# Moving matmul operands to other SBUF addresses, pairing split parts in one slot, and one wide multiply in the last norm

## The chip, the cores and the metric

The kernel runs on one core of a Trainium2 chip. The metric is the device time of one execution in microseconds (us), the median of several runs. Four engines compute: TensorE (PE in the profile; its weight loads are PEld), VectorE (DVE), ScalarE (ACT) and GpSimd (POOL). SyncE (SP) issues the DMAs.

## The reference, cut to what matters

One layer of a streaming encoder over 2048 prompt tokens and 32 sample tokens, width 1024, all in fp32:

```python
qa, ka, va, qb, kb, vb = split_proj(rmsnorm(h, g_attn), w_in)   # one projection, 3072 columns
oa = diff_attn(qa, ka, va, t5_table, lam)     # 4 heads: softmax map 1 minus lam * softmax map 2
ob = band_attn(qb, kb, vb, band_table)        # 8 heads, each 64-token chunk sees itself and 8 before
h = h + concat(rmsnorm(oa, subln_g), rmsnorm(ob, out_norm_b)) @ w_out
c = rmsnorm(h, g_mlp)
h = h + square(relu(c @ w_up)) @ w_down       # 4096 hidden
h = h + sigmoid(h @ w_ple_gate) * (p @ w_ple_proj)
y = rmsnorm(h, g_final)
```

The keys and values are outputs too.

## The kernel before

**Split operands.** Every large product is done in three passes of a fast fp32 format (`F32R`): each fp32 operand is split by `split` (L177, L182, L188) into a high part (a rounded copy, by ScalarE) and a low part (the rest, by GpSimd or VectorE). `mm3` (L220 to L222) then runs high x high, high x low and low x high into the same PSUM tile. Each matmul has a *stationary* operand (128 x 128, loaded by a weight load) and a *moving* operand (128 partitions x up to 512 columns). So nearly every tile in this text comes as a pair of parts.

**Tokens** are tiled in four blocks of 512, the last of 544 (512 + 32), which is worked as two halves of 272 (`SUBS`). Stages in order:

- *Projection* (`vwide`, `vtile`, `proj`). In `vwide` and `vtile`, which make the values, the activations `aH`, `aL` are stationary and the weights move: 512 columns wide in `vwide` (weight tiles `wh0`, `wl0`), 256 wide in `vtile` (weight tiles `wh`, `wl` of shape 4 x 256). In `proj`, which makes queries and keys, the weights are stationary and `aH`, `aL` move.
- *Attention* (`attn_a_pair`, `attn_b_pair`). Scores `s` move the keys `ka` or `kbt`. The weighted sum `o` of `attn_a_pair` (L723 to L725) has the values `v` stationary and the transposed probabilities `pH`, `pL` moving, 256 wide; `attn_b_out` (L883) moves `pb`, 512 wide.
- *Output projection and MLP* for blocks 0 and 1 (`outproj`, `mlp`), whose moving operands are in the pools `actq`, `hq` and `uq`; then for blocks 2 and 3, where `mlp7` computes the first MLP product with seven half-size products instead of eight (operands `cs`, made by `cparts`, or by `cstage` through DRAM and `cload`). From `oload(2, ...)` on, the parts `ou` (attention outputs), `hu` (gate input), `uh`, `ul` (MLP hidden) and `pT` are in the pool `uh` with its ring tag `u`.
- *Gate* (`gate`) and *last norm* (`final`) for each block, woven into the MLP of another block; those of block 3 end the program.

The order of the work on each engine is fixed when the program is built, by a scheduler that simulates times and gives out slots of the pools. A new tile waits for the release of the slot that it takes.

**Addresses.** A pool's bytes per partition are the sum of its rings (tag by tag, in order of first use, `bufs` slots each, rounded up to 32 bytes). Pools opened on the left are stacked upwards from the low end, pools with `side="right"` downwards from the top. Two tiles exist for their size alone: `edge` (24 floats, topmost on the right, so that the first right-hand pool ends at 229,248) and `round` (24 floats at the low end). The sums give these places; the *phase* is the start address modulo 256 bytes:

| moving operand | pool | start | phase |
|---|---|---|---|
| `wh0`, `wl0`, 512 wide | `wv0`, right | 159,328 + 2,048 i | 96 |
| `wh`, `wl`, 256 wide | `wp`, left, slots of 4,096 | 11,264 + 1,024 i | 0 |
| `pH`, `pL`, 256 wide | `a0` at 155,264; `a1` at 155,520, right | 206,720; 196,736 | 128 |
| `pb`, 512 wide | `b` at 156,672, right | 204,416 | 128 |
| `ou`, `hu`, `uh`, `ul`, `pT` | `uh`, right, 20 slots of 2,176 | 185,728 + 2,176 i | 0 and 128 in turn |
| `cs` of block 2, 256 wide | `cs`, right, slots of 4,352, 16 floats in | 75,968 | 192 |
| `cs` of block 3, 272 wide | `cs`, right | 75,904 + 1,088 k | 128, 192, 0, 64 |
| `aH`, `aL` (blocks 0 to 2), `cH`, `cL`, `hH`, `hL` | left | multiples of 256 | 0 |

**Last norm.** For each half of block 3 `final` has the eight tiles of `h` (1024 = 8 x 128 rows) multiplied by the scale `y`: tile 7 by VectorE (L1405), tiles 6 and 5 by GpSimd (`pool_tt`, L167), tiles 4 to 0 one by one by VectorE (L1413); tiles 4 to 7 go out in one DMA, tiles 0 to 3 in another.

Of the kernel before, what the change touches and what calls it, by code (L numbers as in the profile page):

```python
# [13 lines left out]
F32 = mybir.dt.float32  # L14
# [6 lines left out]
P = 128  # L21
# [13 lines left out]
BLK = 544  # L35
# [107 lines left out]


class Kern:
    def __init__(self, tc, a):
        self.tc = tc
        self.nc = tc.nc
        self.a = a
        self.nt = 3  # L150
        self.pieces = None

    def dma(self, dst, src):
# [455 lines left out]
    def attn_a_pair(self, g, j, ka, ba, pool, ps_s, ps_t, ps_o, late, first=None):  # L609
# [72 lines left out]
        for c0 in range(0, len(kts), 4):  # L682
            ch = kts[c0 : c0 + 4]
            v = pool.tile([P, 4, 2, P], F32R, tag="v", bufs=2, name="v")
            if samp:
                for i, kn in ch:
                    self.dma(
                        v[:kn, i].rearrange("p a b -> p (a b)"),
                        self.vS[0][SP + P * i : SP + P * i + kn, 256 * g : 256 * g + 256],
                    )  # L690
            else:
                nch = len(ch)
                ins = self.dma(
                    v[:, :nch].rearrange("p k a b -> p k (a b)"),
                    self.vS[0][P * c0 : P * (c0 + nch), 256 * g : 256 * g + 256].rearrange("(k p) c -> p k c", p=P),
                )
                if c0 == 8 and late:
                    with self.tc.issue_after(ins.ins):
                        late.pop(0)()
            pH = pool.tile([P, 4, 256], F32R, tag="pH", bufs=2, name="pH")  # L700
            pL = pool.tile([P, 4, 256], F32R, tag="pL", bufs=2, name="pL")
            for qi, w in enumerate(ws):
                nr = SS if samp else P
# [92 lines left out]
    def attn_b_pair(self, h, j, kt, v, kb, bb, q, t1, pool, ps_s, ps_t, ps_o, step, late):  # L796
# [9 lines left out]
        for qi, t in enumerate(tiles):  # L806
# [37 lines left out]
            def second(qi=qi, nr=nr, kts=kts, held=held, end=t is tiles[-1]):  # L844
                if qi == 0:
                    px.append(pool.tile([P, 6, 2, 256], F32R, tag="p", bufs=2, name="pb"))
                p = px[0]
                e = held[0]
# [65 lines left out]
    def oload(self, b, wk, up, out, r=None):  # L914
# [74 lines left out]
    def cparts(self, b, wk, cs, out, r):  # L989
# [34 lines left out]
    def cstage(self, b, up, out, r):  # L1024
# [5 lines left out]

        def parts(k, *which):
            for x, raw in which:
                t = up.tile([P, up.aw], F32R, tag="u", name="cst")[:, :n]
                self.split(t[:, :m], t[:, m:], raw, "act", "dve")
                self.dma(out[x][:, :, k], t.rearrange("p (i c) -> p i c", i=2))
# [134 lines left out]
    def mlp7(self, b, hh, box, ops, wk, up, mm, md):  # L1170
# [83 lines left out]
        for ch in range(DFF // (2 * P)):  # L1254
# [4 lines left out]
            for f in range(2):  # L1259
                us.append([up.tile([P, up.aw], F32R, tag="u", name=x)[:, :n] for x in ("uh", "ul")])  # L1260
            r0, r1 = tmp("r0", n), tmp("r1", n)
# [22 lines left out]
    def hparts(self, b, wk, up, out):  # L1284
        n, t0 = BN[b], 512 * b
        hH, hL = [[up.tile([P, BLK], F32R, tag="u", name="hu")[:, :n] for k in range(8)] for _ in range(2)]
        out.append((hH, hL))
# [7 lines left out]
    def ptile(self, b, up, wk):  # L1295
        n, t0 = BN[b], 512 * b
        pT = [[up.tile([P, up.aw], F32R, tag="u", name="pT") for _ in range(2)] for _ in range(2)]
        for k in range(2):
            raw = (
                up.tile([P, up.aw], F32, tag="u", name="praw") if wk is None  # L1300
                else wk.tile([P, BLK], F32, tag="tmp", bufs=self.nt, name="praw")
# [5 lines left out]
    def gate(self, b, h, up, act, md, wk=None, made=None, pT=None):  # L1307
# [13 lines left out]
        else:  # L1321
            hH, hL = [[up.tile([P, BLK], F32R, tag="u", name="hu")[:, :n] for k in range(8)] for _ in range(2)]
        if made is None:
            for k in range(8):
                self.split(hH[k], hL[k], h[:, k, :n], "act", "dve" if k % 2 else "pool")
        for dq in range(2):
            ph, pl = self.wunit(a["w_ple_proj"][dq], [2, 512])
            for d4 in range(4):
                d = 4 * dq + d4
                wh, wl = self.wunit(a["w_ple_gate"][d], [8, P])  # L1330
                for s0, sn in SUBS[b]:
# [5 lines left out]
                    sg = (  # L1337
                        up.tile([P, up.aw], F32, tag="u", name="sig") if wk is None
                        else wk.tile([P, BLK], F32, tag="tmp", bufs=self.nt, name="sig")
# [28 lines left out]
    def final(self, b, h, wk, mm):  # L1368
# [22 lines left out]
        for s0, sn in SUBS[b]:  # L1391
# [14 lines left out]
            for k in range(6, -1, -1):  # L1406
                hv = h[:, k, sub]
                if not end:
                    nc.vector.scalar_tensor_tensor(hv, hv, self.g_final[:, k : k + 1], y, op0=ALU.mult, op1=ALU.mult)  # L1409
                elif k in (5, 6):  # L1410
                    self.pool_tt(hv, hv, y, ALU.mult)
                else:
                    nc.vector.tensor_tensor(hv, hv, y, op=ALU.mult)  # L1413
# [296 lines left out]
```

## Time and profile before

| | |
|---|---|
| median of 3 runs | 3025.55 us (3023.77 to 3027.49) |
| the profiled execution | 3025.88 us, of which its span is 3023.8 us |
| mean granted TensorE clock | 0.990 |
| TensorE busy | 2925.0 us, 97% of the span, 17217 matmuls |
| GpSimd, VectorE, ScalarE busy | 1887.1, 1823.2, 1746.1 us |

The span runs from the first to the last instruction. [...]

### The profile page before, as it was taken

Reading aid. Unit: us, or ns where it says so; the run is one execution under the profiler, and the core shown is the slowest. Engines: PE = TensorE matmul, PEld = TensorE weight load, DVE = VectorE, ACT = ScalarE, POOL = GpSimd, SP = SyncE. Lnnn points to the kernel's source line nnn. Section 1 sums busy time; section 2 is a strip of 40 time slices with the busy share of each in tenths; the row PEclk is TensorE's granted clock in tenths of the full one; section 3 lists DMA queues with packets and bytes.
Section 4 is the critical chain, followed back from the end, with each engine's and each line's share of the span. In section 5 each row is a group of like instructions: output and inputs, shape, how many; then the busy total and the mean of one; then the engine's idle time right before and its main releaser. Section 6 shows DMA issues by size and latency. Waiting matters only on the chain. (4 is left out here: it accounts for less than half of the span.)

```text
span 3023.8 us, 49919 instructions
## 1 busy us (share of the span) xinstructions
PE 2925.0 (97%) x17217; PEld 2576.6 (85%) x17217; DVE 1823.2 (60%) x4217; ACT 1746.1 (58%) x3226; POOL 1887.1 (62%) x2509
## 2 busy tenths in 40 slices
PE   8999999999989999999999999999999999999997
PEld 6798889999877888888888888778788887999997
DVE  5256554676565554667566566445677885677664
ACT  5365554777666665655665655554655455555455
POOL 2568775323465444666655655787688888787774
PEclk9999999999999999999999999999999999999999
DMA  9877867987887453655643543446423446323231
GB/s 311 283 235 237 242 205 220 272 238 223 251 251 219 136 152 105 188 150 168 207 143 124 149 141 111 157 157 209 162 91 134 142 142 239 129 91 119 98 103 54
DMA packets 295204, 528.45 MB, mean 175 GB/s; under 512 B 36316, under 2 KB 159232, under 8 KB 294952
## 3 DMA queue, kind: packets, MB, share of 16 engines
q1 hardware_dynamic: 294952, 525.27, 55.7%
q8 instruction: 136, 2.23, 0.3%
q14 instruction: 116, 0.95, 0.1%
HBM read 424.66 MB, written 104.45 MB: 175 GB/s over the span
## 5 line engine op out<-in xcount | busy, mean ns | idle before, releaser
L177 POOL TENSOR_TENSOR wl<-wr,wh 128x256 fp32r<-128x256 f32 x632 | 472.0, 780 | 246.2 <-ACT wh L182 218.3
L182 ACT ACTIVATE piece<-wr 128x512 fp32r<-128x512 f32 x406 | 245.4, 624 | 290.4 <-PE ups L221 131.2
L177 POOL TENSOR_TENSOR piece<-wr,piece 128x256 fp32r<-128x256 f32 x404 | 338.2, 862 | 93.5 <-ACT piece L182 87.0
L182 ACT ACTIVATE wh<-wr 128x1024 fp32r<-128x1024 f32 x228 | 240.0, 1055 | 200.2 <-PE ups L221 42.6
L167 POOL TENSOR_TENSOR wl<-wr,wh 128x256 fp32r<-128x256 f32 x280 | 216.6, 805 | 202.1 <-ACT wh L182 199.9
L220 PE MATMUL dps<-uh,piece 128*128 128x272 f32 (+1 forms) x768 | 246.7, 325 | 10.3 <-ACT piece L182 6.8
L167 POOL TENSOR_TENSOR piece<-wr,piece 128x256 fp32r<-128x256 f32 x280 | 237.2, 879 | 18.2 <-ACT piece L182 14.9
L222 PE MATMUL dps<-uh,piece 128*128 128x272 f32 (+1 forms) x768 | 247.1, 324 | 1.5 <-POOL piece L167 1.0
L221 PE MATMUL dps<-ul,piece 128*128 128x272 f32 (+1 forms) x768 | 247.0, 323 | 0.1
L221 PE MATMUL ups<-cs,piece 128*128 128x256 f32 (+1 forms) x864 | 244.8, 283 | 0.0
L220 PE MATMUL ups<-cs,piece 128*128 128x256 f32 (+1 forms) x864 | 244.8, 283 | 0.0
L222 PE MATMUL ups<-cs,piece 128*128 128x256 f32 (+1 forms) x864 | 244.7, 284 | 0.0
L220 PE MATMUL qps<-aH,wh 128*128 128x512 f32 (+1 forms) x640 | 227.4, 356 | 5.8 <-DVE ql L502 4.2
L221 PE MATMUL qps<-aL,wh 128*128 128x512 f32 (+1 forms) x640 | 227.2, 355 | 0.0
L222 PE MATMUL qps<-aH,wl 128*128 128x512 f32 (+1 forms) x640 | 226.7, 355 | 0.0
L665 ACT ACTIVATE e<-e,nm 128x128 f32<-128x128 f32 (+16 forms) x136 | 157.2, 1156 | 109.6 <-DVE nm L663 109.1
L1150 DVE TENSOR_TENSOR h<-h,dps 128x512 f32<-128x512 f32 x256 | 173.1, 681 | 69.0 <-PE dps L222 67.8
L1193 DVE TENSOR_TENSOR h<-h,dps 128x272 f32<-128x272 f32 (+1 forms) x384 | 188.8, 513 | 42.3 <-PE dps L222 41.7
L220 PE MATMUL dps<-uh,wh 128*128 128x512 f32 x512 | 204.7, 400 | 5.6 <-DVE h L1150 4.5
L220 PE MATMUL ups<-cH,wh 128*128 128x512 f32 x512 | 202.5, 396 | 0.0
L222 PE MATMUL ups<-cH,wl 128*128 128x512 f32 x512 | 202.3, 395 | 0.0
L221 PE MATMUL ups<-cL,wh 128*128 128x512 f32 x512 | 202.2, 395 | 0.0
(312 smaller groups left out, 9139.7 us busy)
## 6 DMA issues: line engine op xcount, KB each, us to landing
wr<-w_up SPq DMA_DIRECT2D x128, 512.0 KB, 3.5
wr<-w_down SPq DMA_DIRECT2D x128, 512.0 KB, 3.5
q<-qS SPq DMA_DIRECT2D x128, 256.0 KB, 5.2
v<-vSa SPq DMA_DIRECT2D x64, 512.0 KB, 4.6
wr<-w_qk SPq DMA_DIRECT2D x50, 512.0 KB, 5.0
ka<-kS SPq DMA_DIRECT2D x32, 512.0 KB, 7.4
wr<-w_out SPq DMA_DIRECT2D x32, 512.0 KB, 4.5
wr<-w_ple_gate SPq DMA_DIRECT2D x32, 512.0 KB, 4.1
```

What stands on the lines that cost most here:

```text
L167: nc.gpsimd.tensor_tensor(out[:, sl], a[:, sl], b[:, sl], op=op)
L177: nc.gpsimd.tensor_tensor(out[:, sl], a[:, sl], b[:, sl], op=op)
L182: nc.scalar.activation(hi, raw, AF.Copy)
L220: nc.tensor.matmul(ps, lh, rh, start=start and i == 0, stop=False)
L221: nc.tensor.matmul(ps, lh, rl, start=False, stop=False)
L222: nc.tensor.matmul(ps, ll, rh, start=False, stop=stop and i == n - 1)
L665: nc.scalar.activation(row, row, AF.Exp, bias=nmx, accum_out=z[:nr, m : m + 1])
L1150: nc.vector.tensor_tensor(hv, hv, ps, op=ALU.add)
L1193: nc.vector.tensor_tensor(hv, hv, ps, op=ALU.add)
```

## The change

The `edge` tile grows from 24 to 56 floats, so every right-hand pool begins lower. Unused gap tiles are put ahead of and behind `pH`, `pL` in the pools of `attn_a_pair` (48 and 80 floats) and of `pb` in that of `attn_b_pair` (96 and 32 floats), and 120 floats ahead of `xt` in `pp0`. `wh` and `wl` get slots of 4,608 bytes, in which a 4 x 256 tile starts 48 floats in. `cs` operands of block 2 start 48 floats into their tile instead of 16. The ring `u` of pool `uh` has 10 slots of 4,608 bytes instead of 20 of 2,176: a new class `Even` gives both parts of a split tile out of one slot, at floats 64 and 576 for widths to 512, at 32 and 608 for 544. A tile that is no part of a pair (`praw`, `sig`) takes a whole slot. In the last norm of block 3 GpSimd scales tiles 5 and 4, VectorE tiles 7 and 6, and then tiles 0 to 3 in one instruction with `y` broadcast.

```diff
+def pairs(up, count, w, name):
+    if isinstance(up, Even):
+        t = [up.pair(w, F32R, name) for _ in range(count)]
+    else:
+        t = [[up.tile([P, w], F32R, tag="u", name=name) for _ in range(2)] for _ in range(count)]
+    return [[p[i] for p in t] for i in range(2)]
+
+class Even:
+    whole = False
+    def __init__(self, pool, aw):
+        self.pool, self.aw = pool, aw
+    def pair(self, w, dt, name):
+        t = self.pool.tile([P, 1152], dt, tag="u", name=name)
+        return [t[:, o : o + w] for o in ((32, 608) if w > 512 else (64, 576))]
+    def tile(self, shape, dt, tag, name):
+        return self.pair(shape[1], dt, name)[0]
...
-            hi = self.wp.tile([P] + shape, F32R, tag="wh", bufs=3, name="wh")
-            lo = self.wp.tile([P] + shape, F32R, tag="wl", bufs=3, name="wl")
+            o = 48 if shape == [4, 256] else 0
+            hi, lo = [
+                self.wp.tile([P, 1152], F32R, tag=x, bufs=3, name=x)[:, o : o + 1024].rearrange(
+                    "p (k c) -> p k c", c=shape[1]
+                )
+                for x in ("wh", "wl")
+            ]
...
+                pool.tile([P, 48], F32, tag="gap0", bufs=1, name="gap")
             pH = pool.tile([P, 4, 256], F32R, tag="pH", bufs=2, name="pH")
             pL = pool.tile([P, 4, 256], F32R, tag="pL", bufs=2, name="pL")
+                pool.tile([P, 80], F32, tag="gap1", bufs=1, name="gap")
...
+                        pool.tile([P, 96], F32, tag="gap0", bufs=1, name="gap")
                     px.append(pool.tile([P, 6, 2, 256], F32R, tag="p", bufs=2, name="pb"))
+                        pool.tile([P, 32], F32, tag="gap1", bufs=1, name="gap")
...
-            oact = [[up.tile([P, up.aw], F32R, tag="u", name="ou")[:, :n] for k in range(8)] for _ in range(2)]
+            oact = pairs(up, 8, n, "ou")
...
-            ops[x] = [t[:, 16 : 16 + 4 * m].rearrange("p (k c) -> p k c", c=m) for t in tiles]
+            ops[x] = [t[:, 48 : 48 + 4 * m].rearrange("p (k c) -> p k c", c=m) for t in tiles]
...
+                if not t:
+                    t = up.pair(n, F32R, "cst")
+                p = t.pop(0)
-            for i in range(2):
-                tmp = up.tile([P, up.aw], F32, tag="u", name="ct")[:, :n]
+            for i, tmp in enumerate(up.pair(n, F32, "ct")):
...
-                elif k in (5, 6):
+                elif k in (4, 5):
                     self.pool_tt(hv, hv, y, ALU.mult)
-                else:
+                elif k == 6:
                     nc.vector.tensor_tensor(hv, hv, y, op=ALU.mult)
+                elif k == 0:
+                    hv = h[:, :4, sub]
+                    nc.vector.tensor_tensor(hv, hv, y.unsqueeze(1).broadcast_to((P, 4, sn)), op=ALU.mult)
...
-            opened(top, "edge", 1, side="right").tile([P, 24], F32, name="edge")
+            opened(top, "edge", 1, side="right").tile([P, 56], F32, name="edge")
+                pp.tile([P, 120], F32, tag="gap", bufs=1, name="gap")
-            up = Sized(opened(top, "uh", 20, side="right"), BLK)
+            up = Even(opened(top, "uh", 10, side="right"), BLK)
```

More of the change, by code (lines that the diff above doesn't have):

```diff
@@ L699, in attn_a_pair @@
                         late.pop(0)()
+            fresh = pool is not self.spaced
+            if fresh:
+                self.spaced = pool
+                pool.tile([P, 48], F32, tag="gap0", bufs=1, name="gap")
             pH = pool.tile([P, 4, 256], F32R, tag="pH", bufs=2, name="pH")
             pL = pool.tile([P, 4, 256], F32R, tag="pL", bufs=2, name="pL")
+            if fresh:
+                pool.tile([P, 80], F32, tag="gap1", bufs=1, name="gap")
             for qi, w in enumerate(ws):
@@ L845, in second @@
                 if qi == 0:
+                    fresh = pool is not self.spaced
+                    if fresh:
+                        self.spaced = pool
+                        pool.tile([P, 96], F32, tag="gap0", bufs=1, name="gap")
                     px.append(pool.tile([P, 6, 2, 256], F32R, tag="p", bufs=2, name="pb"))
+                    if fresh:
+                        pool.tile([P, 32], F32, tag="gap1", bufs=1, name="gap")
                 p = px[0]
@@ L1031, in parts @@
         def parts(k, *which):
+            t = []
             for x, raw in which:
-                t = up.tile([P, up.aw], F32R, tag="u", name="cst")[:, :n]
-                self.split(t[:, :m], t[:, m:], raw, "act", "dve")
-                self.dma(out[x][:, :, k], t.rearrange("p (i c) -> p i c", i=2))
+                if not t:
+                    t = up.pair(n, F32R, "cst")
+                p = t.pop(0)
+                self.split(p[:, :m], p[:, m:], raw, "act", "dve")
+                self.dma(out[x][:, :, k], p.rearrange("p (i c) -> p i c", i=2))
         late = ()
@@ L1259, in mlp7 @@
             for f in range(2):
-                us.append([up.tile([P, up.aw], F32R, tag="u", name=x)[:, :n] for x in ("uh", "ul")])
+                us.append(up.pair(n, F32R, "uh"))
             r0, r1 = tmp("r0", n), tmp("r1", n)
@@ L1285, in hparts @@
         n, t0 = BN[b], 512 * b
-        hH, hL = [[up.tile([P, BLK], F32R, tag="u", name="hu")[:, :n] for k in range(8)] for _ in range(2)]
+        hH, hL = pairs(up, 8, n, "hu")
         out.append((hH, hL))
@@ L1296, in ptile @@
         n, t0 = BN[b], 512 * b
-        pT = [[up.tile([P, up.aw], F32R, tag="u", name="pT") for _ in range(2)] for _ in range(2)]
+        pT = pairs(up, 2, n, "pT")
         for k in range(2):
             raw = (
-                up.tile([P, up.aw], F32, tag="u", name="praw") if wk is None
+                up.tile([P, n], F32, tag="u", name="praw") if wk is None
                 else wk.tile([P, BLK], F32, tag="tmp", bufs=self.nt, name="praw")
@@ L1321, in gate @@
         else:
-            hH, hL = [[up.tile([P, BLK], F32R, tag="u", name="hu")[:, :n] for k in range(8)] for _ in range(2)]
+            hH, hL = pairs(up, 8, n, "hu")
         if made is None:
@@ L1337, in gate @@
                     sg = (
-                        up.tile([P, up.aw], F32, tag="u", name="sig") if wk is None
+                        up.tile([P, sn], F32, tag="u", name="sig") if wk is None
                         else wk.tile([P, BLK], F32, tag="tmp", bufs=self.nt, name="sig")
```

1 line of the change is left out of this document (added).

## The prediction

> **What bounds the kernel now.** I read first the busy times, the slices and the chain of the page:
>
> ```profile
> PE 2925.0 (97%) x17217; PEld 2576.6 (85%) x17217; DVE 1823.2 (60%) x4217; ACT 1746.1 (58%) x3226; POOL 1887.1 (62%) x2509
> PE   8999999999989999999999999999999999999997
> PE 19%; POOL 3%; DVE 1%; DMA 1%; issue 1%; ACT 1%; SPq 0%; DVEq 0%; POOLq 0%; ACTq 0%
> ```
>
> TensorE is busy 97% of the span, in every slice, and it is nearly the whole of what the chain lists; the other engines are busy about 60%. The change takes no matmul away. So what it can do to the middle of the kernel is to change the pitch of a matmul, the time from its start to the next one's start. I then looked for stretches that hold one kind of matmul without a stall, with the view of busy time by stretch (its x counts every matmul that touches the stretch, one or two more than start in it):
>
> ```profile
> core 0: us, PE busy (x) PEld busy (x) DVE busy (x) ACT busy (x) POOL busy (x), PEclk, DMA share, GB/s
> 39.93:56.27 16.34, 16.34 (x72) 13.14 (x70) 10.41 (x26) 10.60 (x23) 0.00 (x0) 1.00 0.83 293
> 134.85:161.62 26.77, 26.77 (x119) 22.16 (x118) 5.52 (x15) 7.09 (x13) 14.14 (x20) 1.00 0.59 211
> 150.00:640.00 490.00, 474.33 (x3163) 434.86 (x3162) 290.33 (x860) 295.59 (x619) 295.82 (x422) 0.99 0.79 236
> 448.02:455.26 7.24, 7.24 (x62) 7.24 (x62) 4.61 (x8) 4.45 (x10) 6.99 (x10) 1.00 0.69 214
> 1200.00:1900.00 700.00, 697.16 (x3637) 592.56 (x3636) 437.62 (x1027) 422.03 (x652) 414.27 (x578) 1.00 0.51 153
> 1875.22:1877.98 2.76, 2.76 (x25) 2.76 (x23) 1.18 (x2) 0.60 (x1) 2.63 (x4) 1.00 0.27 97
> 1982.04:1987.26 5.22, 5.22 (x25) 4.32 (x24) 3.09 (x3) 2.98 (x6) 4.00 (x7) 1.00 0.40 116
> 2015.27:2051.93 36.66, 36.66 (x161) 29.84 (x159) 26.87 (x28) 16.39 (x28) 33.80 (x37) 1.00 0.85 280
> 2174.49:2188.32 13.83, 13.83 (x123) 13.82 (x122) 7.41 (x14) 9.57 (x19) 8.40 (x12) 1.00 0.49 179
> 2467.51:2471.59 4.08, 4.08 (x37) 4.07 (x35) 2.63 (x5) 3.98 (x8) 1.30 (x2) 1.00 0.57 189
> 2557.05:2580.39 23.34, 23.34 (x102) 18.96 (x101) 6.82 (x11) 11.05 (x20) 16.62 (x23) 1.00 0.40 135
> ```
>
> Matmuls 512 columns wide: in `vwide` (39.93) the moving `wh0` has phase 96 and the pitch is 16.34 / 70 = 233.4 ns; in `proj` (134.85) and the gate of block 1 (1982.04) all operands have phase 0 and it is 26.77 / 118 = 226.9 and 5.22 / 23 = 227.0. The output projection (2015.27) and the gate (2557.05) that read pool `uh`, with phases 0 and 128 mixed, take 36.66 / 159 = 230.6 and 23.34 / 101 = 231.1, though the second is the same loop as the gate at 1982. Matmuls 256 wide: `vtile` (448.02), phase 0, 7.24 / 61 = 118.7; `o` (1875.22), phase 128, 2.76 / 23 = 120.0; `cs` (2174.49), phase 192, 13.83 / 122 = 113.4, and in a busier stretch (2467.51) 4.08 / 35 = 116.6. All at full granted clock. So phase and pitch go together, by 3% to 5%.
>
> These are different stages, so I looked for a contrast inside one. The 272-wide `cs` matmuls of block 3 go through all four phases, three matmuls each, in every product:
>
> ```profile
> 2580.63 0.29 PE L220 MATMUL ups<-cs,lead 128*128 128x272 f32 x1
> ...
> 2581.01 0.28 PE L220 MATMUL ups<-cs,lead 128*128 128x272 f32 x1
> ...
> 2581.38 0.29 PE L220 MATMUL ups<-cs,lead 128*128 128x272 f32 x1
> ...
> 2581.76 0.28 PE L220 MATMUL ups<-cs,lead 128*128 128x272 f32 x1
> ...
> 2582.13 0.29 PE L220 MATMUL ups<-cs,lead 128*128 128x272 f32 x1
> ...
> 2926.66 0.29 PE L220 MATMUL ups<-cs,piece 128*128 128x272 f32 x1
> ```
>
> Phases 128, 192, 0, 64: the threes take 0.38, 0.37, 0.38, 0.37 us. Over the 370 threes without a stall from the first of these rows to the last, the starts give 379.4 ns at 128, 380.1 at 0, but 375.2 at 192 and 375.8 at 64. With stage and weights the same, 64 and 192 are 1.5 ns a matmul quicker. The sign agrees; the size is smaller than 4 to 6 ns.
>
> **The change part by part.** The new addresses are sums of tile sizes. `edge` takes 128 bytes more, so right-hand pools end at 229,120. Pool `a0` grows by 512 bytes to 74,496 and begins at 154,624; `pH` lies 51,456 + 192 further, at 206,272, phase 192; in `a1` likewise 196,288, phase 192; `v`, stationary, goes from 128 to 0. `wv0` begins at 142,336, so `wh0` starts at 158,720, phase 0. `wh` at 11,264 + 192 has phase 192. Pool `uh` begins at 183,040: parts 512 wide at phase 0, 544-wide ones at 128, their second halves at 192. `cs` of block 2: the pool begins at 73,216, and 192 bytes further the phase is 192 as before. `pb`: 204,160, still 128. What counts, by form:
>
> ```profile
> L222 PE MATMUL vps<-wh,aL 128*128 128x256 f32 x384 | 108.5, 284 | 0.0
> L222 PE MATMUL vps<-wh,aL 128*32 128x256 f32 x32 | 9.2, 287 | 0.0
> L723 PE MATMUL o<-pH,v 128*128 128x256 f32 x256 | 73.1, 285 | 0.9 <-ACT pH L716 0.7 <-DMA v<-vSa 0.2
> L220 PE MATMUL vps<-wh,aH 128*128 128x512 f32 x64 | 26.8, 421 | 8.9 <-ACT wh L182 8.9
> L222 PE MATMUL dps<-uh,piece 128*128 128x512 f32 x256 | 101.0, 397 | 1.5 <-POOL piece L167 1.0
> L220 PE MATMUL gps<-hu,piece 128*128 128x512 f32 x128 | 52.2, 411 | 8.0 <-ACT piece L182 5.6 <-DVE hd L961 1.9 <-DVE sig L1345 0.5
> L220 PE MATMUL ops<-ou,piece 128*128 128x512 f32 x64 | 26.2, 409 | 2.9 <-ACT piece L182 2.9
> L220 PE MATMUL pps<-pT,piece 128*128 128x512 f32 x32 | 12.9, 405 | 0.0
> ```
>
> Each row is one of `mm3`'s three passes, so counts are times 3.
>
> *256 wide, to phase 192.* `vtile` 3 x (384 + 32) = 1248, `o` 3 x 256 = 768. The new pair of phases (moving 192, stationary 0) is that of `cs`, so I take the middle of its two pitches, 115.0: 1248 x 3.7 + 768 x 5.0 = 4.6 + 3.8 = 8.4 us. Bounds: 1.5 ns, from the threes, gives 3.0; the quiet 113.4 gives 6.6 + 5.1 = 11.7. [...]
>
> *`wh0`, to phase 0.* 3 x 64 = 192 matmuls, 233.4 to 226.9: 1.2 us; nothing, if weights arriving set that stage.
>
> *Pool `uh`, 512 wide, all to phase 0.* 3 x (256 + 128 + 64 + 32) = 1440 matmuls at 231. The same loop at phase 0 has 227.0. In `uh` itself the few matmuls with phase 0 before and behind them look no quicker than the rest, so I take three quarters of the difference: 1440 x 3 = 4.3 us; bounds 0 and 1440 x 4 = 5.8.
>
> *Costed at nothing.* 272-wide `uh`: four phases become 128 and 192, whose threes average what the four do. `cs` of block 3 still has all four. `pb` keeps its phase. The keys `ka` in `a0` also go from 128 to 0; few matmuls of full width read them there, and I leave them out. The gaps issue nothing.
>
> *Pairs.* The ring keeps its capacity for pairs: 20 single slots or 10 double ones. `praw` and `sig` waste a half. `cstage` used nine singles a step, and now five doubles.
>
> *The last norm.* This is on the chain at the end:
>
> ```profile
> 3011.89 2.88 DVE h L1413 x5
> 3016.11 1.10 DVE h L1405
> 3018.12 1.41 DVE h L1413 x4
> ...
> 3001.12 0.73 DVE L1383 TENSOR_TENSOR sqy<-sqy,ysq 128x544 f32<-128x544 f32 x1 [0.72 <-ACT ysq L1378]
> 3006.33 0.43 DVE L1383 TENSOR_TENSOR sqy<-sqy,ysq 128x272 f32<-128x272 f32 x1
> 3016.16 1.67 POOL L167 TENSOR_TENSOR h<-h,ry 128x272 f32<-128x272 f32 x2 [2.74 <-DVE ry L1403]
> 3017.13 2.40 DVE L1413 TENSOR_TENSOR h<-h,ry 128x272 f32<-128x272 f32 x5
> ```
>
> Five multiplies take 2.40 us, 0.48 each. 272 columns cost 0.43 and 544 cost 0.73, so 1088 in one are estimated at 0.73 + 2 x 0.30 = 1.33. One of 0.48 and one of 1.33 replace five: 0.6 us saved in each half, both on the chain, so 1.1 us (bounds 0, if the wide one costs four single ones, and 1.2). GpSimd still does two, ending at 3017.83, before VectorE in either order; the DMA of tiles 4 to 7 now waits for its second, and is hidden by the later DMA of tiles 0 to 3.
>
> Sum: 8.4 + 1.2 + 4.3 + 1.1 = 15.0 us. TensorE is busy 474.33 of 490 us where `vtile` runs and 697.16 of 700 where most of `o` runs, so nearly all of it shortens the span; I take off 0.5 for the idle 3%. The profiled execution took 3025.88 us, 0.3 over the median of 3025.55, so 3025.9 - 14.5 = 3011.4. At the low bounds 3.0 + 0 + 0 + 0 gives 3023; at the high ones 11.7 + 1.2 + 5.8 + 1.2 = 19.9 gives 3006.
>
> **The rivals.** *The address does not count.* The pitches would then be those of the stages, by what other engines and weight loads do there, and only the norm gains: 3025.9 - 1.1 = 3024.8. For it: those few phase-0 matmuls in `uh`, and a weight-load row that is full in `vtile` (7.24 of 7.24). Against: it is as full in `cs` (13.82 of 13.83) at 113.4, the two gates run one loop at 227 and 231, and the threes differ within one product. [...]
>
> *Pairs run short, and the kernel gets slower.* A double slot comes free only when both parts are done, and `cstage`'s go out by DMA:
>
> ```profile
> L182 ACT ACTIVATE cst<-ct x28: 412/414/419, 2359.8 to 2516.0; 128x272 fp32r<-128x272 f32 x28
> DMA to landing us min/median/max: 2.6/4.1/5.6
> ```
>
> Between 2338 and 2519 the `uh`, `ul` pair of a chunk takes a slot beside them, two chunks in flight: 4 + 5 = 9 of 10 slots. If one chunk's pair waits a landing, 4.1 us, in each of the eight half-steps, TensorE's down products behind it stand still for up to 33 us: 3011.4 + 33 = 3044. It cancels the gain from 1.9 us a half-step on (15 / 8). Against: before, 8 + 9 = 17 of 20 were in use at the same points, and no row of the waits shows a wait for these DMAs.
>
> **How the numbers follow.** What a measurement of this kernel can tell from no change is about 0.2%, 6 us, so faster means under 3019.8. The forecast has 0.74 and spreads from 3006 to 3023, with 0.05 of it above 3019.8; no address effect 0.13 (3024.8); pairs run short 0.09 (3032 to 3044); a gain beyond my bounds, through fewer clock drops or idle, 0.04. Faster: 0.69 + 0.04 = 0.73; same: 0.05 + 0.13 = 0.18; slower 0.09. The likeliest case gives 3011.4; its own range is 3006 to 3020. To leave out no more than 2 in 10 the range takes in the second case: 3005 to 3025.
>
> **What would show it.** Right: `vtile` and `o` stretches at 113 to 117 ns, the stretch of `vwide` at 227, the gate on `hu` at 227 to 229, `cs` of block 2 unchanged at 113 to 117, and the last norm with 2 instead of 5 multiplies in about 1.8 us. Wrong: the same pitches at the new phases; or TensorE waits for `uh` or `ul` that the chain did not have, between 2338 and 2519.

## The result and the profile after

Over 13 runs each, the kernel after takes 3017.16 us (median; 3011.11 to 3025.36) and the kernel before 3024.95 (3019.89 to 3032.13). The ratio is 0.9976, with a 95% interval of 0.9965 to 0.9987: 7.8 us faster by the medians, 3.9 to 10.6 by the interval. The forecast was 14.5.

The profiled execution of after took 3012.5 us, 13.4 less than that of before. It is one of the quicker ones. The runs spread with the mean granted clock: 3011.11 and 3013.29 us at 0.992 and 0.993, 3023.34 and 3020.16 at 0.987. In the trace of before the clock is granted at half for 47.8 us ahead of the last norm, in nine windows of 3.4 to 10.2 us, and in that of after for 37.5. In such a window of before (2142.91 to 2153.15 us, granted 0.50) a 512-wide matmul without a stall takes 426 to 427 ns instead of 227 to 233. So by an estimate half of the 10.3 us, about 5 of the 13, belongs to these two executions and not to the change. What follows goes by pitches in stretches at full clock.

The page of after, busy times and the chain:

```profile
PE 2913.4 (97%) x17217; PEld 2571.6 (85%) x17217; DVE 1829.5 (61%) x4211; ACT 1744.5 (58%) x3226; POOL 1882.9 (63%) x2509
PE 15%; DVE 1%; DMA 0%; ACT 0%; issue 0%; POOL 0%; DVEq 0%; SPq 0%
```

TensorE has the same 17217 matmuls and is still nearly all of what the chain lists. Busy time by stretch, for stretches with one kind of matmul and no stall, as in the prediction (the intervals that I divide by are counted from the start times, for the matmuls' records overlap: those of before last 387 to 398 ns in the stretches of the output projection and the gate, with 227 to 233 from start to start):

```profile
42.70:57.67 14.97, 14.97 (x67) 12.39 (x66) 7.44 (x18) 5.25 (x13) 0.00 (x0) 1.00 0.46 176
253.45:256.51 3.06, 3.06 (x29) 3.06 (x27) 3.06 (x5) 2.17 (x4) 2.89 (x3) 1.00 0.96 304
446.20:449.04 2.84, 2.84 (x27) 2.84 (x26) 2.81 (x10) 2.08 (x6) 1.48 (x2) 1.00 0.69 200
1301.41:1304.12 2.71, 2.71 (x25) 2.71 (x23) 0.98 (x2) 0.28 (x1) 0.04 (x1) 1.00 0.45 172
1370.89:1373.53 2.64, 2.64 (x25) 2.64 (x24) 1.32 (x4) 0.28 (x1) 2.23 (x4) 1.00 0.03 10
2007.74:2038.84 31.10, 31.10 (x138) 25.71 (x137) 20.32 (x24) 12.14 (x23) 24.07 (x26) 1.00 0.81 280
2107.45:2112.66 5.21, 5.21 (x24) 4.32 (x23) 4.48 (x5) 1.35 (x3) 5.21 (x6) 1.00 1.01 357
2161.44:2175.81 14.37, 14.37 (x123) 14.37 (x122) 9.09 (x16) 10.51 (x22) 9.74 (x13) 1.00 0.50 175
2161.44:2512.40 350.96, 340.98 (x2120) 303.61 (x2119) 268.92 (x406) 186.31 (x357) 284.50 (x328) 1.00 0.42 145
```

`vwide` (42.70) went from 233.4 to 14.97 / 66 = 226.8 ns, the output projection on `uh` (2007.74) from 230.6 to 31.10 / 137 = 227.0, the gate on `hu` (2107.45) from 231 to 5.21 / 23 = 226.5. `vtile` has two paces, 3.06 / 26 = 117.7 and 2.84 / 25 = 113.6, and so has `o`, 2.71 / 23 = 117.8 and 2.64 / 23 = 114.8. The row that was not forecast is 2161.44: the first stretch of `cs` of block 2, whose address phase did not change, went from 113.4 to 14.37 / 122 = 117.8. The last row spans that whole stage, from its first `cs` matmul to the next gate. In before it was:

```profile
2174.49:2524.40 349.91, 339.29 (x2120) 300.38 (x2119) 270.19 (x404) 184.96 (x355) 286.67 (x329) 1.00 0.43 146
```

Before 349.91 us, after 350.96, the same 2120 matmuls at full clock: in the stage that holds 768 of the 1440 `uh` matmuls nothing was gained, though they became quicker. (Of the 1440, those of the down products are called `u` below.)

The last norm of after, timeline of VectorE and of GpSimd (start, duration, instruction):

```profile
2998.04 0.44 DVE L1445 SCALAR_TENSOR_TENSOR ry<-sqy,ry 128x272 f32<-128x272 f32 x1
2998.52 0.50 DVE L1447 SCALAR_TENSOR_TENSOR h<-h,g_final_s,ry 128x272 f32<-128x272 f32 x1
2998.94 1.00 DVE L1455 TENSOR_TENSOR h<-h,ry 128x272 f32<-128x272 f32 x1
2999.86 1.84 DVE L1458 TENSOR_TENSOR h<-h,ry 128x1088 f32<-128x1088 f32 x1
...
2998.65 1.89 POOL L190 TENSOR_TENSOR h<-h,ry 128x272 f32<-128x272 f32 x2 [17.99 <-DVE ry L1445]
```

In before the column `ry` of the second half is

```profile
3015.64 0.44 DVE L1403 SCALAR_TENSOR_TENSOR ry<-sqy,ry 128x272 f32<-128x272 f32 x1
```

and the five multiplies start at 3017.13 and take 2.40. From the end of `ry` to the end of the last multiply it is 3.22 us in after (2998.48 to 3001.70) and 3.45 in before (3016.08 to 3019.53). That is 0.2 us saved a half instead of 0.6: the single multiply takes 1.00 us, all of it while GpSimd multiplies, and the wide one 1.84, the first 0.7 of it (until 3000.54) beside GpSimd.

### The profile page after: what moved, and what is told of

Its sections match the earlier page's. It is cut to its first block, busy times and chain, and to the rows that moved or that the text cites. A ratio compares the mean times of both kernels' runs of the same rounds, so it can differ in the third digit from the quotient of the medians.

```text
span 3010.7 us, 49898 instructions
## 1 busy us (share of the span) xinstructions
PE 2913.4 (97%) x17217; PEld 2571.6 (85%) x17217; DVE 1829.5 (61%) x4211; ACT 1744.5 (58%) x3226; POOL 1882.9 (63%) x2509
## 5 line engine op out<-in xcount | busy, mean ns | idle before, releaser
L248 PE MATMUL dps<-uh,piece 128*128 128x272 f32 (+1 forms) x768 | 244.9, 323 | 9.6 <-ACT piece L205 5.5
L250 PE MATMUL dps<-uh,piece 128*128 128x272 f32 (+1 forms) x768 | 247.5, 325 | 1.9 <-POOL piece L190 1.6
L249 PE MATMUL dps<-uh,piece 128*128 128x272 f32 (+1 forms) x768 | 246.3, 322 | 0.1
L249 PE MATMUL qps<-aL,wh 128*128 128x512 f32 (+1 forms) x640 | 227.1, 355 | 0.0
L250 PE MATMUL qps<-aH,wl 128*128 128x512 f32 (+1 forms) x640 | 226.7, 354 | 0.0
```

The source lines that it names most:

```text
L248: nc.tensor.matmul(ps, lh, rh, start=start and i == 0, stop=False)
L249: nc.tensor.matmul(ps, lh, rl, start=False, stop=False)
L250: nc.tensor.matmul(ps, ll, rh, start=False, stop=stop and i == n - 1)
```

## The experiments

The table gives the mean pitch in ns over all matmuls of a group that are followed without a stall (the next start within 238 ns for 512 columns, within 132 for 256), from the start times in the traces. The pair in brackets is the phase of the moving and of the stationary operand (mixed where the moving ones have phases 0 and 128). `hu` is the gate, `u` the down products of block 2, `ou` its output projection.

```
run                  vtile 256        hu 512           u 512            ou 512  cs 256 of block 2
before               118.9 (0,0)      231.6 (mixed)    231.0 (mixed)    230.6   115.4 (192,0)
after                115.6 (192,0)    227.1 (0,0)      227.4 (0,0)      227.0   117.6 (192,0)
e1_shared_mixed      119.0 (0,0)      232.7 (mixed)    230.7 (mixed)    233.1   116.2 (192,0)
e2_phase128          116.7 (64,0)     232.4 (128,0)    233.0 (128,0)    231.6   114.4 (192,0)
e3_cs64              118.5 (128,0)    227.1 (0,0)      228.9 (0,0)      227.0   117.8 (64,0)
e4_cs0               118.0 (160,0)    227.3 (0,0)      229.4 (0,0)      226.9   119.5 (0,0)
f1_uh64_norm         115.4 (192,0)    227.2 (0,0)      230.4 (64,0)     227.1   117.4 (192,0)
f2_uh192_pb00        115.5 (192,0)    227.0 (0,0)      232.9 (192,0)    226.9   115.1 (192,0)
f3_pieces128         115.5 (192,0)    232.3 (0,128)    231.3 (0,128)    231.5   117.4 (192,128)
f4_pieces64          115.4 (192,0)    233.3 (0,64)     233.3 (0,64)     233.3   118.4 (192,64)
g1_best_candidate    115.7 (192,0)    227.2 (0,0)      232.9 (192,0)    227.1   114.4 (192,0)
g2_uh_mixed          115.5 (192,0)    229.9 (mixed)    230.6 (mixed)    232.5   116.3 (192,0)
g3_both128           115.5 (192,0)    227.4 (128,128)  228.8 (128,128)  226.9   117.9 (192,128)
g4_norm_no_gpsimd    115.5 (192,0)    226.9 (0,0)      227.2 (0,0)      227.0   117.5 (192,0)
```

The bound of 238 leaves out intervals of 240 and 241 ns in e2, e3, f3 and g3; with them `hu`, `u` and `ou` of f3 are at 232.4 to 232.8, and `u` of e3 and of g3 at 229.5.

Theories: P, the moving operand's own phase sets the pitch; S, not the address but the shared slots and the order that comes with them; P2, only a change of phase from one matmul to the next costs; D, the difference between moving and stationary phase counts; M, a pace that a stretch takes over from the matmuls ahead of it, so that `cs` gives back what `u` gains.

**Shared slots, old phases.** The first run keeps the slots and mixes the phases, with `vtile` at 0 and `o` at 64:

```diff
-        return [t[:, o : o + w] for o in ((32, 608) if w > 512 else (64, 576))]
+        return [t[:, o : o + w] for o in ((32, 608) if w > 512 else (64, 608))]
...
-            o = 48 if shape == [4, 256] else 0
+            o = 0 if shape == [4, 256] else 0
...
-                pool.tile([P, 48], F32, tag="gap0", bufs=1, name="gap")
+                pool.tile([P, 16], F32, tag="gap0", bufs=1, name="gap")
...
```

> From the changed kernel: shared slots are kept, but the low part of a 512-wide pair starts at phase 128 (floats 64 and 608) as half of the operands did before; vtile's moving weights go back to phase 0 in their larger slots; pH and pL go from phase 192 to 64. The three stages are read apart. Theory P (a matmul's pitch follows the phase of its own moving operand): 512-wide matmuls of pool uh 231 ns (changed kernel 227), vtile 119 (115.6), o 115 to 117 as at 192. Theory S (the gain comes from the shared slots and the other order of work, not from the phase): uh stays at 227, vtile at 115.6, o at 119.5 or unchanged. Theory M (at phase 64 or 192 a 256-wide stretch has two pitches, 113 and 118, and keeps the one that the matmuls before it set): as P, and the cs products of block 2, whose own phase stays 192, come back from 117.6 to about 115.4, because the 512-wide matmuls between them have mixed phases again; by P and S cs stays at 117.6. Time by P and M: 3 x 1.9 + 4.1 = about 10 us over the changed kernel, less 3 if cs recovers.

The rows of its `vtile` and its first `cs` stretch:

```profile
175.46:179.77 4.31, 4.31 (x37) 4.31 (x37) 2.61 (x10) 2.56 (x6) 2.29 (x5) 1.00 1.05 296
2172.90:2186.75 13.85, 13.85 (x123) 13.85 (x122) 8.10 (x15) 9.79 (x19) 9.10 (x12) 1.00 0.50 179
```

`vtile` is back at 4.31 / 36 = 119.7, `hu` and `ou` at 232.7 and 233.1. S falls: with the slots of after and the old phases the old pitches return. And `cs`, untouched, is back at 13.85 / 122 = 113.5 in this stretch, and at 116.2 over all. The run took 3023.89 us beside 3023.70 of before.

**All at 128.** Both parts of a pair at phase 128, `vtile` at 64, `o` at 128, `pb` at 0:

```diff
+        return [t[:, o : o + w] for o in ((32, 608) if w > 512 else (32, 608))]
...
+            o = 16 if shape == [4, 256] else 0
...
+                pool.tile([P, 32], F32, tag="gap0", bufs=1, name="gap")
...
+                        pool.tile([P, 64], F32, tag="gap0", bufs=1, name="gap")
...
```

> From the changed kernel: both parts of a 512-wide pair in pool uh at phase 128; vtile's moving weights at phase 64; pH and pL back at phase 128; pb at phase 0 instead of 128. P: uh 231 (as pb, which has phase 128 throughout, has 230.5), vtile 115 to 116, o 119.5 (changed kernel 117.1 in a1), pb 227 to 229 instead of 230.5. A rival P2 (only a change of phase between successive matmuls costs, not the phase): uh stays at 227, pb at 230.5. S: nothing of this moves. M adds: cs, at 192 as before, takes another mixture of 113 and 118 than 117.6, either way.

3021.63 us. A constant phase of 128 is as slow as a mixed one, so P2 falls. `o` returns to 118.7 and 119.1, `pb` doesn't get better at moving phase 0 (231.4, its stationary operand at 128), which P had wrong. `cs` is at 114.4, its best.

**`cs` at 64 and at 0.** The next two move `cs` (and `vtile` to 128 and 160; the first also puts `pb` at 64, 544-wide pairs at 0, so that their halves start at 0 and 64, and takes the last norm back, the second puts `wh0` at 64):

```diff
-            ops[x] = [t[:, 48 : 48 + 4 * m].rearrange("p (k c) -> p k c", c=m) for t in tiles]
+            ops[x] = [t[:, 16 : 16 + 4 * m].rearrange("p (k c) -> p k c", c=m) for t in tiles]
...
```

This is e3; e4 has `0 : 0 + 4 * m`.

> From the changed kernel: cs operands of block 2 at phase 64 (192); vtile's moving weights at 128; pb at 64 (128); the 544-wide pairs of pool uh at 0 and 64 instead of 128 and 192; and the last norm as before the change (tiles 5 and 6 by GpSimd, five single multiplies by VectorE). P: cs 113 to 118, vtile 119, 272-wide dps unchanged at 125 within 0.5, pb open (no 512-wide operand has had phase 64). M: cs stays near 117.6, since the 512-wide matmuls around it are those of the changed kernel. Norm: if the wide multiply brought 0.2 us a half, as the two traces show, five multiplies take 2.4 us and the chain from the last ry on 3.4 us, 0.2 more than 3.2; if it brought 0.6 as I had forecast, 0.6 more.

> From the changed kernel: cs operands of block 2 at phase 0; vtile's moving weights at phase 160; wh0, wl0 of vwide at phase 64 (0; 96 before the change). P: cs 119 to 120, as 256-wide operands at phase 0 or 128 have elsewhere, so 1344 x 2 ns = 2 to 3 us more; M the same; S: cs stays at 117.6. vwide: 228 at phase 0 and 233 at 96; if any multiple of 64 bytes will do, 228 at 64, if only even ones, 231 to 233. vtile at 160: if odd multiples of 32 are as bad as 96 was for wh0, 119 or more; if only the distance from 0 and 128 counts, 115 to 116.

`cs` goes to 117.8 at 64 and 119.5 at 0, `vtile` to 118.5 and 118.0, `wh0` to 229.5, `pb` to 232.5. So the 256-wide groups were slowest at 0 and 128, `vtile` at 118.9 and 118.5, `cs` at 119.5 (0), `o` at 118.7 to 119.5 (128), as the forecast had it; 160 is hardly better. `u`, whose own phases stay (0,0), slows down from 227.4 to 228.9 and 229.4 when `cs` alone moves in its stage, as `cs` went from 117.6 to 116.2 and 114.4 when `u` moved in e1 and e2. The last norm of e3, with five single multiplies again, takes 3.46 us from the end of `ry` on, beside 3.45 in before. One execution each took 3026.78 and 3019.43 us, 7 us apart, which is less than the 14 us over which the runs of after spread.

**`u` at 64 and 192, and the norm without GpSimd.**

```diff
-        return [t[:, o : o + w] for o in ((32, 608) if w > 512 else (64, 576))]
+        return [t[:, o : o + w] for o in ((32, 608) if w > 512 else (16, 592) if name == "uh" else (64, 576))]
...
-                elif k in (4, 5):
-                    self.pool_tt(hv, hv, y, ALU.mult)
-                elif k == 6:
...
-                elif k == 0:
...
+                elif k in (0, 4):
+                    m = 4 - k // 4
...
```

This is f1, whose norm is in two multiplies, three and four tiles wide. f2 has `(48, 624)` for `uh`, moves `pb` and `vbt` to phase 0 and leaves the norm as in after.

> From the changed kernel: only the MLP hidden parts of block 2 (uh, ul, 512 wide) start at phase 64; ou, hu and pT stay at 0. And the last norm without GpSimd: VectorE multiplies tiles 4 to 6 and tiles 0 to 3 in two wide instructions. Theory M (what the down products of pool uh gain by their phase, the cs products between them lose): dps 229 to 231 instead of 227.4 (wh0 at phase 64 has 229.5 against 228.2), cs 114.5 to 116 instead of 117.6, their sum, about 350 us in the stage, unchanged within 1. If instead cs depends on uh only through phases 0 and not 0, cs 114.4 as with uh at 128, dps 229, and the sum falls by 2 to 3 us. Norm: if the wide multiply of 1.84 us was held up by GpSimd's multiplies, the one of tiles 0 to 3 takes 1.3 us here, the other 1.0, and from the last ry on VectorE needs 2.9 instead of 3.2 us a half; if a wide multiply with y broadcast is slow of itself, it stays at 1.8.

> From the changed kernel: uh, ul of block 2 at phase 192; and pool b 128 bytes lower, so that in ob both the moving pb and the stationary vbt have phase 0 (so far, moving and stationary: 128 and 0 gave 231.0, 128 and 128 230.5, 0 and 128 231.4, 64 and 128 232.5). P: ob at 0 and 0 227 to 228.5, as other 512-wide operands have; if the pitch of ob has another cause (runs of seven matmuls, each with its own wait), 230 to 232 again. uh at 192: M says dps 230 to 233 and cs below 117, sum unchanged within 1.

For the 512-wide `u` 64 and 192 are no help: 230.4 and 232.9, beside 227.4 at 0. At 192, `cs` behind them falls to 115.1. At 64 it stays at 117.4, where M had 114.5 to 116 and an unchanged sum: here `u` lost 768 x 3.0 = 2.3 us of pitch and `cs` gave back 0.2, so M fails in this run. `pb` with both operands at 0 is at 230.0. 3012.89 and 3014.48 us beside 3021.89 of before; the norm is read below.

**The stationary operand moved instead.** Gap tiles put the weight pieces at phase 128 and at 64; every moving operand stays:

```diff
             self.wp = opened(top, "wp4", 6)
+            self.wp.tile([P, 32], F32, tag="gap", bufs=1, name="gap")
...
```

This is f3; f4 has 16 floats.

> From the changed kernel: only the stationary weight pieces of blocks 2 and 3 move, from phase 0 to 128; all moving operands keep their phases. P (only the moving operand's phase counts): gps, ops, pps, dps stay at 227, cs at 117.6. Theory D (the difference between moving and stationary phase counts, since both are read at the same time): 512-wide at 0 against 128 gets 231 to 232, as 128 against 0 has; cs at 192 against 128 behaves as 64 against 0, 117.8; 272-wide dps 125.5 to 126.2 as with uh at 0 and 64 against 0. Time by D about 7 us over the changed kernel, by P none.

> From the changed kernel: the stationary weight pieces of blocks 2 and 3 at phase 64 instead of 0. P: nothing moves. D: 512-wide 0 against 64 is as 192 against 0, not yet measured in gps, 229 to 232; cs 192 against 64 is as 128 against 0, 118.5 to 120.

All 512-wide matmuls on these pieces are slow again, 231 to 232 in the table and 233.3, with moving operands still at phase 0. P in its simple form falls. `cs` goes to 117.4 at (192,128) and 118.4 at (192,64), near the 117.8 and 118.5 that 256 columns have at (64,0) and (128,0) in e3, as D said. D's reason, that both operands are read at the same time, no run shows; the profile shows only that weight loads and matmuls run side by side, 25.81 us of the one within 31.83 of the other in the row of f3 below. The two executions took 3020.73 and 3021.05 us beside the same 3021.89 of before. Last, both operands at 128:

```diff
+        return [t[:, o : o + w] for o in ((32, 608) if w > 512 else (96, 608))]
```

This comes on top of the gap tiles of f3.

> The pieces of the weights at phase 128, as in the third run of the second set, and now both parts of the 512-wide pairs at phase 128 too: moving and stationary operand at the same phase, which isn't 0. Theory D (the difference of the two phases counts): 227 ns again for hu, ou and pT. Rival (both must start at phase 0, as the 230.4 ns of pb and the 230.6 of ka at 128 with 128 suggest): 230 to 233 ns.

The same 138 matmuls of the output projection, in e1, e2, f3, f4 and then in this run:

```profile
2016.81:2048.77 31.96, 31.96 (x138) 25.73 (x137) 21.40 (x24) 13.10 (x23) 26.54 (x29) 1.00 0.81 276
```

```profile
2016.37:2048.20 31.83, 31.83 (x139) 25.81 (x138) 20.80 (x24) 12.98 (x23) 25.57 (x28) 1.00 0.81 268
```

```profile
2015.75:2047.58 31.83, 31.83 (x139) 25.81 (x138) 21.29 (x24) 13.09 (x23) 25.81 (x28) 1.00 0.81 270
```

```profile
2013.13:2045.10 31.97, 31.97 (x139) 25.62 (x138) 20.80 (x25) 13.59 (x24) 26.09 (x28) 1.00 0.81 277
```

```profile
2010.98:2042.05 31.07, 31.07 (x138) 25.71 (x137) 21.37 (x24) 12.99 (x23) 25.13 (x27) 1.00 0.79 266
```

31.83 to 31.97 us at (mixed,0), (128,0), (0,128) and (0,64), but 31.07 at (128,128), as the 31.10 of after at (0,0). D holds in these groups as far as they were moved: the output projection is at 226.9 to 227.1 ns where both operands start at the same phase, 0 or 128, and at 231.5 to 233.3 in these four runs. (My rival had taken the 230.4 of `pb` at (128,128) as a sign against it; that group is at 230.0 at (0,0) too, so something else holds it.) In the timing g3 has a ratio to before of 0.9973 (0.9961 to 0.9984).

**The pairs alone undone, and `cs` behind them.**

```diff
+        return [t[:, o : o + w] for o in ((32, 608) if w > 512 else (64, 608))]
```

> After with one edit: the second part of a 512-wide pair starts at phase 128 instead of 0, as about a third of them did before the change, so that phases 0 and 128 alternate. All else of the change stays. Theory P: the uh, hu, ou and pT matmuls go back to 231 to 233 ns, 384 x 5.6 + 768 x 3.5 + 192 x 6 + 96 x 6 ns = 6.6 us slower than after. Theory M: cs goes back to 115 to 116 ns and gives back 2 to 3 of it: 3 to 4.5 us slower than after, so 3 to 5 us faster than before. Rival (the pairs' share of the gain is nothing, all of it is in the 256-wide matmuls): as after.

0.9967 (0.9952 to 0.9982), median 3017.80: no slower than after. P's 6.6 us would have made it 0.9998, above the interval; M's 3 us, 0.9986, lie a little above it too, but after's own interval reaches to 0.9987, so of the 3 us these runs can't decide. Four rows of this kernel show how a gain can be returned, two pairs of a `u` stretch and the `cs` stretch that follows:

```profile
2208.36:2211.11 2.75, 2.75 (x13) 2.25 (x12) 2.47 (x6) 2.29 (x4) 0.64 (x1) 1.00 0.01 3
2211.34:2215.46 4.12, 4.12 (x37) 4.12 (x35) 3.05 (x6) 4.04 (x8) 3.71 (x5) 1.00 0.36 123
2229.47:2232.27 2.80, 2.80 (x13) 2.25 (x12) 2.36 (x6) 2.77 (x6) 2.60 (x4) 1.00 0.00 0
2232.50:2236.49 3.99, 3.99 (x36) 3.98 (x35) 2.89 (x5) 3.76 (x8) 3.59 (x4) 1.00 0.39 128
```

12 intervals of `u` at 2.75 / 12 = 229, then 35 of `cs` at 4.12 / 35 = 117.7; 12 at 2.80 / 12 = 233, then 35 at 3.99 / 35 = 114.0. The operands have the same phases in both. Of its twelve `cs` stretches behind `u`, the four behind 228.8 to 228.9 run at 117.7 to 117.8, the seven behind 233.3, and one behind a stall, at 114.0 to 114.1. In e1 it is the same for the eleven without a stall ahead. In after every `u` stretch is at 226.7 to 228.8, and fourteen of fifteen `cs` stretches at 117.7 to 117.8; the other, at 114.1, is behind a `u` stretch with a wait in it. But in g2 `u` itself has two paces with the same phases, 229 with `cs` at 117.7 before and behind it, 233 with `cs` at 114 to 116: these rows show that the paces come in pairs, and not which selects the other.

**The candidate**, with `u` at 192, `pb` at (0,0) and the norm without GpSimd, and **the norm alone**:

> After with three edits: the parts of u of block 2 at phase 192 (the pitch of the uh matmuls was 232.9 ns there, 227.4 at phase 0, and that of the cs matmuls behind them 115.1 instead of 117.6), pb of attention b with both operands at phase 0, and the last norm without GpSimd. Theory M (what the 768 uh matmuls lose, 768 x 5.5 ns = 4.2 us, the 1344 cs matmuls give back, 1344 x 2.5 ns = 3.4 us): equal to the run with the norm alone within 1.5 us. Theory P alone (each group's pitch hangs on its own phases, and cs would stay at 117.6): 4.2 us slower than the run with the norm alone.

> After with one edit: the last norm's multiplies all on VectorE, a wide one of 128x816 and one of 128x1088, and none on GpSimd. Theory (the wide multiply took 1.84 us instead of 1.33 because GpSimd worked beside it): the two take 2.2 us together, a half ends 2.7 us after the column of ry instead of 3.2, 1.1 us less than after in all, 8 to 10 us less than before. Rival (1.84 is VectorE's own pace for this width): 1.4 and 1.84 us, a half 3.7 us, 1 us slower than after.

0.9960 (0.9947 to 0.9973), median 3013.24, and 0.9954 (0.9936 to 0.9972), median 3011.47: equal within their intervals, as M said, but that does not tell M apart (see the stage as a whole, below), and P's 4.2 us (0.9968) would lie in the candidate's interval too. Both are ahead of before; whether they beat after is not settled, for their intervals overlap with its own. Rows of the candidate:

```profile
2168.37:2182.74 14.37, 14.37 (x123) 14.36 (x122) 8.93 (x16) 10.34 (x21) 9.69 (x13) 1.00 0.50 177
2195.09:2199.05 3.96, 3.96 (x19) 3.20 (x18) 2.90 (x6) 3.86 (x8) 1.44 (x2) 1.00 0.32 114
2199.78:2203.76 3.98, 3.98 (x37) 3.98 (x36) 3.31 (x5) 3.53 (x10) 3.98 (x6) 1.00 0.43 132
```

Its first `cs` stretch, behind the gate at 227, runs at 14.37 / 122 = 117.8; behind `u` at 3.96 / 17 = 233 it runs at 3.98 / 35 = 113.7. One kernel, one operand, one phase, two paces, and they go with the matmuls ahead, whose phases this run moved. The last norm of g4:

```profile
2997.60 0.44 DVE L1445 SCALAR_TENSOR_TENSOR ry<-sqy,ry 128x272 f32<-128x272 f32 x1
2998.07 0.50 DVE L1447 SCALAR_TENSOR_TENSOR h<-h,g_final_s,ry 128x272 f32<-128x272 f32 x1
2998.49 2.20 DVE L1455 TENSOR_TENSOR h<-h,ry 128x816 f32<-128x816 f32 x2
```

2.20 us for seven tiles, three in one instruction and four in the next, and 2.65 from the end of `ry`. With GpSimd taking two of the seven, after needs 3.22. Leaving GpSimd out saves 0.57 a half, more than the change's wide multiply had brought.

**The stage as a whole.** All fourteen traces together answer what none of the runs was made for: whether the stage from the first `cs` matmul of block 2 to the next gate follows its matmuls at all. In us, the pitches of `u` and `cs` times their counts, 768 and 1344, and the length of the stage:

```
run      before after  e1     e2     e3     e4     f1     f2     f3     f4     g1     g2     g3     g4
matmuls  332.5  332.7  333.3  332.6  334.1  336.8  334.7  333.6  335.4  338.3  332.6  333.4  334.2  332.5
stage    349.9  350.9  350.3  350.6  350.4  350.3  350.6  350.9  350.7  351.1  351.8  350.7  350.9  350.4
```

```profile
2168.27:2519.33 351.06, 344.83 (x2120) 304.79 (x2119) 268.93 (x405) 186.32 (x355) 284.10 (x328) 1.00 0.43 146
```

It hardly does. This row is f4: its matmuls need 5.8 us more than those of before, its stage is 1.2 longer, and TensorE's idle time has shrunk from 10.6 us to 6.2. In e4 it is 4.3 and 0.4, and f2 has 3.4 us at half clock in this stage and is no longer for it. What the matmuls lose or win, the waits give back. Nearly all the waits, 10.2 of the 10.6 us in before and 9.6 of the 10.0 in after, lie in the last 214 us of the stage, where the operands of block 3 are made beside it. By these rows a slower or quicker `u` would have left the stage at 350 to 352 us with or without an answer of `cs`. So the times of g1 and g4 can't decide between M and P, and of P's 6.6 us in g2 the 2.7 of `u` fall in this stage as well. What sets the length was not tried; of the 10.0 us idle in after, the profile puts 5.5 down to waits for weight pieces that ScalarE splits.

## Why the prediction was right, and where its sizes were off

The direction, the mechanism (pitch goes with address phase) and most signs named in advance came: `vtile` and `o` at 113.6 to 117.8, `vwide` at 226.8, the gate at 226.5. No wait for a pair's slot appeared, and the rival "the address does not count" falls with e1. The size was about twice too large. For 512 columns the forecast went by the phase of the moving operand; that this was enough is luck in part, for the stationary operands happened to lie at phase 0, and f3 makes the same groups slow by moving those alone. By step, in us, with the pitches of the table and the counts of the prediction:

```
step                      forecast  shown
vtile to phase 192             4.6    4.1   1248 x (118.9 - 115.6)
o to phase 192                 3.8    2.0   768 at 118.9/119.5, now 115.6/117.1
wh0 to phase 0                 1.2    1.0   192 x (233.3 - 228.2)
uh 512 wide to phase 0         4.3    5.6   384 x 4.5 + 768 x 3.6 + 192 x 3.6 + 96 x 4.0
uh 272 wide                    0      0.8   1536 x (125.4 - 124.9)
cs of block 2                  0     -3.0   1344 x (115.4 - 117.6)
last norm                      1.1    0.4   2 x 0.2
idle                          -0.5     -
sum                           14.5   10.9
```

- **The step that failed outright is "`cs` of block 2 unchanged at 113 to 117".** I took its two paces, 113.4 and 116.6, for quiet and busy stretches, that is for something of the stage. They are two paces that go with those of the matmuls ahead, and the change moved those. In pitches it cost 3.0 of the 5.6 that `uh` gained, and all of the 2.8 of the `u` products in its own stage.
- **The overlap failed in that stage too.** I let nearly all of the pitch gains shorten the span, because TensorE is busy 474.33 of 490 and 697.16 of 700 us where `vtile` and `o` run. I had not asked the same of the stage of `u`, 768 of the 1440 matmuls and 2.3 of the 4.3 us that I forecast for them. There TensorE is 97% busy as well, but its waits take up what the matmuls lose or win: 349.9 to 351.8 us in every run.
- **The 256-wide term, 8.4, came out at 6.1.** Taking the middle of the two paces, 115.0, was right for `vtile` (115.6) but not for `o` (116.7 over all): most of its stretches go at the slower pace, 117.8. Nothing in the forecast fixed how the paces would mix, so the hit on `vtile` is luck. The start was too high besides, 120.0 in the stretch that I quoted and 118.9 to 119.5 over all.
- **`uh` was undersized**, 5.6 instead of 4.3: I had cut the difference to the other gate by a quarter for a few matmuls at phase 0 that looked no quicker. They stood in stretches of mixed phase, where e1 and g2 show whole stretches at one pace. The stretch at 2557.05 that I read as the gate also holds 21 matmuls on `pT`; the gate alone has 231.6.
- **The last norm, 1.1, came out at 0.4.** (The terms of its sum, twice 0.59, give 1.2.) The two multiplies take 2.76 us instead of the 1.8 named in advance. The estimate of 1.33 for the wide multiply left GpSimd out. Undisturbed, 816 and 1088 columns take 2.20 together; beside GpSimd's two tiles a 272-wide multiply takes 1.00, where `sqy<-sqy,ry` of the same form takes 0.44 in after with GpSimd idle (2997.57).

The 10.9 shown, pitches times counts, lies just above what the runs give, 3.9 to 10.6. What becomes of the other three by the median of 7.8 is open: groups with stalls may have kept theirs in waits, but no run here tells that apart from the clock's spread. `vwide` did not: with its stalls it takes 53.1 us in before and 53.9 in after, but after has a window at half clock in it (22.94 to 26.36 us, granted 0.50); in e2, f1 and g3, with `wh0` at the same phase 0 and no such window there, it takes 52.2.

## What to carry to other kernels

Where TensorE is busy 97% of the span, start addresses are worth reading: sort the matmuls of one form by the start phases of both operands before looking for anything else, and cost a move by the stage's total, not by the group that moves: the group behind may return it, or the stage may wait for something else. A busy share of 97% does not rule that out; a run with slower matmuls shows it, as f4 did here with 5.8 us of pitch for 1.2 of the stage. A group whose pitch has two values in one stage, as `cs` with 114.0 and 117.7 in g2, is a warning that its pace is not set by its own addresses alone. And before two engines share a row of multiplies at the end of a chain, time the one alone: here VectorE alone was 0.57 us a half quicker than VectorE with GpSimd's help.

## What the runs showed of the hardware

- At 512 columns of fp32r the mean pitch in the gate and the output projection was 226.9 to 227.4 ns where moving and stationary operand start at the same phase of 256 bytes, (0,0) or, in g3, (128,128), and 231.3 to 233.3 in these groups and `u` where they don't, at (0,64) in f4, (0,128) in f3, (128,0) in e2 and (192,0) in f2 and g1; (64,0) is milder, 229.5 for `wh0` in e4 and 230.4 for `u` in f1. Other groups with equal phases stay above it: `u` between `cs` stretches, 227.2 to 229.5, `vwide` in after, 228.2, and `pb`, 230.0 at (0,0) and 230.5 at (128,128). The moving phase alone doesn't set it: the matmuls of the output projection that take 31.10 us in after take 31.83 in f3, where the pieces alone are moved, and 31.07 in g3.
- For 256 columns it is not so: (0,0) is the slowest, 118.9 (`vtile` in before) to 119.5 (`cs` in e4) on average, (128,0) has 118.5 (`vtile` in e3) to 119.1 (`o` in e2), and (192,0) is the best, at 113.3 to 114.1 or 117.7 to 117.8 in most long stretches of `cs`.
- Such a pace holds for a whole stretch, in after for 122 matmuls on end, and in after, e1 and g2 goes with the pace of the preceding stretch: `cs` at 117.7 to 117.8 behind `u` at 227 to 229, mostly at 113.3 to 114.1 behind 233. It is not without exceptions: in f2 three of twelve stretches behind 233 run at 117.8, in f1 all twelve behind `u` at (64,0), 230, and in f3, where `cs` has (192,128), all twelve do. The cause of the two paces was not tried, nor whether 256 bytes is the period of the phases.
